# A decoder step: the first projection takes each chunk of tokens through all four channel panels, with both weight panels read side by side

## Chip, cores and metric

The kernel runs on one NeuronCore of a Trainium2 chip. The metric is the device time of one execution in microseconds; the median of the runs counts. The profile is of one further execution.

## The reference

One layer of a decoder for 1024 prompt tokens and 64 sample tokens (8 requests of 8 tokens), all in float32. The part that the change touches is the first 512 columns of the combined input projection, the pooling input `a`:

```python
def rms_norm(x, w):
    x32 = x.astype(F32)
    y = x32 * lax.rsqrt(jnp.mean(jnp.square(x32), axis=-1, keepdims=True) + EPS)
    return y.astype(x.dtype) * w

def project(x, ln1, w_in, q_norm, k_norm):
    p = jnp.einsum('btd,de->bte', rms_norm(x, ln1), w_in)
    a, q, k, v, g_a, g_b = jnp.split(p, IN_SPLITS, axis=-1)      # widths 512, 768, 768, 768, 1024, 1024
    ...
```

After it come the pooling of `a`, three groups of dilated attention, the gates, the output projection and an MLP of width 4096. They are the same before and after.

## The kernel before

**Layout.** Tokens lie along the free dimension (1088 columns), channels along the partitions, in eight k-tiles of 128 (`KD = 8`). The 1088 tokens are cut into three chunks of 384, 384 and 320 columns (`CHUNKS`). The 512 output channels of `a` are four panels of 128; two of them come from one weight panel `i["w_in"][0]` (called a0), two from `i["w_in"][1]` (a1). A weight panel is 128 x 2048 numbers: eight k-tiles of 256 output channels.

**Precision.** Every float32 operand is split into a high and a low part (type `F32R`), and a product is three passes (`PASSES`: high x high, high x low, low x high, weight part first). `split` makes the parts of a weight piece of 512 columns (two k-tiles): a copy on ScalarE (ACT, L116) for the high part, a subtraction on VectorE (DVE, L117) for the low one. `split_x` does the same with x, scaled by the norm's weight `ln1` (ACT L312, VectorE L313), into `act`.

**Buffers.** A weight piece lands in one of three `raw` buffers of 512 columns (`fetch`, L127), so the fourth piece cannot be asked for until the first has been split by both engines. The parts go into one of three `places`, each a whole panel. x lands in `xs`, twelve buffers for the three chunks of four pairs of k-tiles. All of these loads are issued by SyncE (SP) in one order. Accumulators are four PSUM banks.

**Order of the work.** TensorE's order is the program's. The other engines' instructions, SyncE's loads among them, are put in order by a planner that estimates when each can run; it may put a load that can go at once ahead of one that must wait for a buffer. `behind_pe` ties an instruction to the last matmul issued so far, so it can't run sooner.

**The stage.** Twelve small matmuls come first (`wu`). Then a0's four pieces are read (`panel` with `between=first`), after each the next pair of k-tiles of x for chunk 0. TensorE takes chunks 0, 1, 2 through a0 (`pool_input(0, ...)`: pairs of k-tiles, then passes, then the two output panels), and then chunks 0, 1, 2 through a1. After each chunk ACT copies the two accumulators into `ext` (`pool_evac`, L346 and L351). While TensorE works on a1, `x_sums(c)` multiplies the sums of squares of chunk c with a column of ones (L369), which gives the norm of each token; VectorE (L373, L375) and GpSimd (POOL, a power, L374) finish it. The squares are made by `square_x(c)` on ACT (L304), and POOL adds the four pairs of k-tiles with three adds for each chunk (L306). `sample_rows` copies the 64 sample columns with sixteen VectorE casts (L284). `wk` is a small transpose (L444). Right behind the stage stands the q projection of the sample tokens (`pq`, L632), which needs the casts, and the product `mt` (L405), which needs all norms. The next three weight panels (q, k, v) use the free place, then a0's, then a1's.

Of the kernel before, what the change touches and what calls it, by code (L numbers as in the profile page):

```python
# [7 lines left out]
F32 = mybir.dt.float32  # L8
F32R = mybir.dt.float32r
AF = mybir.ActivationFunctionType  # L10
ALU = mybir.AluOpType
# [4 lines left out]
P = 128  # L16
D = 1024
SEQ = 1024
NB, NT = 8, 8
TOK = SEQ + NB * NT  # L20
KD = D // P
CH = 384
# [5 lines left out]
HD = 64  # L28
# [9 lines left out]
def decoder_step(ctx, tc, i, o):  # L38
    nc = tc.nc
    v_, s_, g_, t_ = nc.vector, nc.scalar, nc.gpsimd, nc.tensor  # L40
    dma = nc.sync.dma_start
# [7 lines left out]
    def rr(p, shape, dt, name, tag, bufs):  # L49

        n = turn[p, tag] = turn.get((p, tag), -1) + 1
        return p.tile(shape, dt, name=name, tag=f"{tag}.{n % bufs}", bufs=1)
# [3 lines left out]
    cst = cp.tile([P, i["consts"].shape[1]], F32, name="cst")  # L56
# [8 lines left out]
    ident, m1, m3, halves, hmask, icnt, ms0, ms1, hsel, bsel = (take(n) for n in (128, 256, 128, 64, 1, 15, 136, 136, 4, 4))  # L65
    ln1, ln2, pscale, wqc = cols[:, 0:8], cols[:, 8:16], cols[:, 16:20], cols[:, 20:26]
# [24 lines left out]
    def part4(c):  # L91

        return slice(CHUNKS[c][0] // 4, (CHUNKS[c][0] + CHUNKS[c][1]) // 4)
# [12 lines left out]
    def from4(t, sub="p r l -> p l r"):  # L106
        return t.rearrange("p (r l) -> p r l", r=4).rearrange(sub)
# [7 lines left out]
    def split(dst_hi, dst_lo, src):  # L115
        ins = s_.activation(dst_hi, src, AF.Copy)  # L116
        v_.tensor_tensor(dst_lo, src, dst_hi.bitcast(F32), op=ALU.subtract)  # L117
        return ins

    def fetch(src, name, a, tied=False):  # L120
        raw = rr(wp, [P, 512], F32, name=f"raw_{name}_{a}", tag="raw", bufs=3)
        if callable(src):
            ins = dma(raw.rearrange("p (k n) -> p k n", k=4), src(a))
            if tied:
                behind_pe(ins)
        else:
            dma(raw, src[:, a:a + 512])  # L127
        return raw
# [35 lines left out]
    def panel(src, name, between=None, after=None):  # L164

        n = src.shape[1]
        wt = places[:, place[0] % 3]
        place[0] += 1
        for a in range(0, n, 512):
            raw = fetch(src, name, a)  # L170
            if between is not None:
                between(a // 512)
            ins = split(wt[:, 0, a:a + 512], wt[:, 1, a:a + 512], raw)
            if after is not None:
                behind_pe(ins, after[a // 512])
        throttle.append(ins)
        return wt

    def by_k(wt, kb=KD):
        return wt.rearrange("p s (k n) -> p s k n", k=kb)  # L180
# [69 lines left out]
    def acc_tile(name, tag="acc", bufs=4):  # L250
        return rr(acc_p, [P, 512], F32, name, tag, bufs)
# [17 lines left out]
    def win(name):  # L269
        return rr(xp, [P, LS], F32, name, "win", 2)  # L270
# [10 lines left out]
    def sample_rows():  # L281
        for s in range(2):
            for k in range(KD):
                behind_pe(v_.tensor_copy(smp_t[:, k, s * NS:(s + 1) * NS].rearrange("p (l r) -> p l r", r=4),  # L284
                                         act4[s][k][:, :, SEQ // 4:].bitcast(F32).rearrange("p r l -> p l r")))
    xs = {}

    def load_x(c, j):
        c0, n = CHUNKS[c]
        x = rr(xq, [P, 2, CH], F32, name=f"xs{c}_{j}", tag="xs", bufs=12)  # L290
        if c + j == 0:

            dma(x[:, 0, :n], i["xT"][:, 0, c0:c0 + n])
            dma(cols, i["cols"])
        else:
            dma(x[:, :, :n], i["xT"][:, 2 * j:2 * j + 2, c0:c0 + n])
        xs[c, "t", j] = x[:, :, :n]
        for k in range(2):
            xs[c, 2 * j + k] = x[:, k, :n]

    def square_x(c):
        t = [xs[c, "t", j] for j in range(4)]
        for j in (3, 0, 1, 2):
            behind_pe(s_.activation(t[j], t[j], AF.Square))  # L304
        for j in range(3):
            g_.tensor_tensor(t[3], t[3], t[j], op=ALU.add)  # L306

    def split_x(c, k):
        c0, n = CHUNKS[c]
        hi, lo = (act4[s][k][:, :, part4(c)] for s in range(2))  # L310
        x = xs[c, k].rearrange("p (l r) -> p r l", r=4)
        s_.activation(hi, x, AF.Copy, scale=ln1[:, k:k + 1])  # L312
        v_.scalar_tensor_tensor(lo, x, ln1[:, k:k + 1], hi.bitcast(F32), op0=ALU.mult, op1=ALU.subtract)  # L313

    def first(j):
        if j:
            load_x(0, j)
        else:
            dma(xs[0, 1], i["xT"][:, 1, :CH])
        split_x(0, 2 * j)  # L320
        split_x(0, 2 * j + 1)

    L = 15 + SEQ
    LS = L + NB * 23
    exts = {}

    def pool_input(ja, wt, c, middle=None):
        c0, n = CHUNKS[c]
        pts = [acc_tile(f"a{2 * ja + m}_{c}") for m in range(2)]
        for k in range(0, KD, 2):  # L330
            for p, (a, b) in enumerate(PASSES):
                for m in range(2):
                    for kk in (k, k + 1):
                        last_mm[0] = t_.matmul(  # L334
                            pts[m][:, :n], wt[:, a, kk, m * P:(m + 1) * P], act4[b][kk][:, :, part4(c)],
                            start=(p == 0 and kk == 0), stop=(p == 2 and kk == KD - 1))
            if middle and k == 4:
                middle()
        return pts

    def pool_evac(ja, c, pts):
        c0, n = CHUNKS[c]
        for m in range(2):
            ext = exts[2 * ja + m]
            npr = min(n, SEQ - c0)
            s_.copy(ext[:, 15 + c0:15 + c0 + npr].rearrange("p (l r) -> p l r", r=4),  # L346
                    from4(pts[m][:, :n])[:, :npr // 4])
            if npr < n:
                new = from4(pts[m][:, :n])[:, npr // 4:].rearrange("p (t q) r -> p q r t", q=2)
                for q in range(2):  # L350
                    s_.copy(ext[:, L:].rearrange("p (b t) -> p b t", b=NB)[:, 4 * q:4 * q + 4, 15:], new[:, q])  # L351

    def open_ext(g):
        exts[g] = rr(xp, [P, LS], F32, name=f"ext{g}", tag="ext", bufs=4)
        v_.memset(exts[g][:, :15], 0.0)
# [3 lines left out]
    for _ in range(12):  # L359
        t_.matmul(wu, ones, ones, start=True, stop=True)  # L360
    load_x(0, 0)
    wt = by_k(panel(i["w_in"][0], "a0", first))
    def x_sums(c):
        n = CHUNKS[c][1]
        rt = [rr(ps, [P, 1], F32, name=f"rt{c}_{b}", tag="rt", bufs=3) for b in range(3)]
        for b in range(3):
            w = min(P, n - b * P)
            for k in range(2):
                t_.matmul(rt[b][:w], xs[c, 6 + k][:, b * P:b * P + w], ones[:, :1], start=(k == 0), stop=(k == 1))  # L369
        for b in range(3):  # L370
            w = min(P, n - b * P)
            col = slice(3 * c + b, 3 * c + b + 1)
            v_.tensor_scalar(xms[:w, col], rt[b][:w], 1.0 / D, EPS, op0=ALU.mult, op1=ALU.add)  # L373
            g_.tensor_tensor(rtok[0][:w, col], xms[:w, col], mhalf[:w, :1], op=ALU.pow)  # L374
            v_.tensor_scalar(xeps[0][:w, col], xms[:w, col], EPS, None, op0=ALU.mult)  # L375
# [33 lines left out]
            v_.tensor_scalar(xeps[g][:, :8], xg, EPS, None, op0=ALU.mult)  # L409

    v_.memset(rtok[0], 0.0)
    for c in range(3):
        if c < 2:
            for j in range(4):
                load_x(c + 1, j)
        if c == 0:
            open_ext(0)
            open_ext(1)
        pool_evac(0, c, pool_input(0, wt, c))
        if c < 2:  # L420
            for k in range(KD):
                split_x(c + 1, k)
        if c:
            square_x(c - 1)
    square_x(2)
    w1 = by_k(panel(i["w_in"][1], "a1"))
    dma(cst, i["consts"])
    v_.tensor_scalar(wqs, wqc, HD ** -0.5, None, op0=ALU.mult)
    dma(states, i["stateT"].rearrange("g p b t -> p g (b t)"))
    kn = win("kn")[:, :P]  # L430
    for g in range(3):
        dma(kn[2 * g:2 * g + 2], i["qk_norm"][g, 1].rearrange("(j d) -> j d", j=2))
    open_ext(2)
    open_ext(3)
    for c in range(3):
        pool_evac(1, c, pool_input(1, w1, c, (lambda: x_sums(2)) if c == 2 else None))
        if c == 0:
            x_sums(0)
            sample_rows()
        if c == 1:  # L440
            x_sums(1)

            wk = rr(ps, [P, 512], F32, name="wk", tag="wu", bufs=1)[:, :6]
            t_.transpose(wk, kn[:6], ident[:6, :6])  # L444
            v_.tensor_tensor(wqk, wqs, wk, op=ALU.mult)
    moving = by_residue()
    next(moving)
    px.close()
# [722 lines left out]
    for g in (2, 1, 0):  # L1171
# [42 lines left out]
        for blks in ((8, 0), (1,), (2,), (3,), (4,), (5,)) + (((6, 7),) if g else ((6,), (7,))):  # L1214
# [12 lines left out]
            for js in (((0, 1), (2,)) if blks[0] in (1, 2, 3, 4, 5) else ((0,), (1,), (2,))):  # L1227
                for b in (blks[::-1] if g < 2 and js == (2,) and 8 in blks else blks):
# [4 lines left out]
                    def middle():  # L1233
                        step()
                        if own:
                            own_step(1)
# [1031 lines left out]
```

## Time and profile before

| | us |
|---|---|
| runs, median (lowest to highest of 3) | 1401.73 (1401.05 to 1402.97) |
| the profiled execution's own time | 1399.09 |
| its span, first to last instruction | 1397.3 |
| TensorE matmul busy | 1390.2 |
| VectorE, ACT, POOL busy | 954.0, 756.1, 258.3 |

The profile's page and its views give times in microseconds from the start of the span. PE is TensorE's matmuls, PEld its weight loads, DVE VectorE, ACT ScalarE, POOL GpSimd, SP SyncE (SPq: its queue, which issues loads). L334 is line 334 of the kernel. In a line of the order of time stand start, length, engine, line, operation, the names of what is written and read, the shape, the count, and in brackets the engine's idle time before it with what ended that. The chain that ended last goes back from the last instruction, at each step to what released it.

### The profile page before, as it was taken

Reading aid. Unit: us, or ns where it says so; the run is one execution under the profiler, and the core shown is the slowest. Engines: PE = TensorE matmul, PEld = TensorE weight load, DVE = VectorE, ACT = ScalarE, POOL = GpSimd, SP = SyncE. Lnnn points to the kernel's source line nnn. Section 1 sums busy time; section 2 is a strip of 40 time slices with the busy share of each in tenths; the row PEclk is TensorE's granted clock in tenths of the full one; section 3 lists DMA queues with packets and bytes.
Section 4 is the critical chain, followed back from the end, with each engine's and each line's share of the span. In section 5 each row is a group of like instructions: output and inputs, shape, how many; then the busy total and the mean of one; then the engine's idle time right before and its main releaser. Section 6 shows DMA issues by size and latency. Waiting matters only on the chain.

```text
span 1397.3 us, 29307 instructions
## 1 busy us (share of the span) xinstructions
PE 1390.2 (99%) x11101; PEld 1341.6 (96%) x11101; DVE 954.0 (68%) x1707; ACT 756.1 (54%) x1787; POOL 258.3 (18%) x362
## 2 busy tenths in 40 slices
PE   9999999999999999999999999999999999999998
PEld 8988987888999999999999999999999999999998
DVE  7788744776876776975559677765665686664565
ACT  8557875787764224554337454554554544444443
POOL 0854356676500000000010000000000000000100
PEclk9999999999999999999999999999999999999999
DMA  6456886755587777956369668765768987777674
GB/s 216 133 166 211 245 246 195 231 139 137 149 248 232 244 220 257 318 194 211 130 199 296 222 217 290 245 204 204 250 202 287 319 274 257 238 239 230 211 256 170
DMA packets 180445, 311.96 MB, mean 223 GB/s; under 512 B 26696, under 2 KB 82318, under 8 KB 178255
## 3 DMA queue, kind: packets, MB, share of 16 engines
q1 hardware_dynamic: 174670, 258.04, 57.8%
q0 software_dynamic: 5632, 52.04, 11.6%
q8 instruction: 87, 1.43, 0.4%
q14 instruction: 56, 0.45, 0.1%
HBM read 239.94 MB, written 122.12 MB: 259 GB/s over the span
## 4 chain that ended last, share of the span: by engine, by line
PE 98%; ACT 0%; DMA 0%; POOL 0%; SPq 0%; issue 0%; DVE 0%; DVEq 0%
PE pz L1330 24%; PE pd L2113 24%; PE pg L1330 12%; PE ph L205 7%; PE pqk L205 6%; PE pab L1330 5%; PE pv L205 5%; PE a L334 3%; PE pk L205 2%; PE pq L205 2%; PE sg0b L702 1%; PE pog0b L735 1%; PE pl L513 1%; PE tpg0b L721 1%; PE sg1b L702 0%; PE tpg1b L721 0%
## 5 line engine op out<-in xcount | busy, mean ns | idle before, releaser
L2113 PE MATMUL pd<-places 128*128 128x272 f32 x2688 | 331.7, 287 | 0.0
L2113 PEld LDWEIGHTS pd<-places 128*128 128x128 f32 x2688 | 331.6, 188 | 0.0
L116 ACT ACTIVATE places<-raw_d 128x544 fp32r<-128x544 f32 (+1 forms) x176 | 110.6, 646 | 159.1 <-DMA raw_d<-z_d 54.8
L2166 POOL DMA_DIRECT2D out_kv_sample_dram<-in_cache_kv_dram x96 | 46.9, 489 | 791.1 <-ACT places L116 582.2
L117 DVE TENSOR_TENSOR places<-raw_d,places 128x544 fp32r<-128x544 f32 (+1 forms) x176 | 122.4, 710 | 90.8 <-ACT places L116 89.0
L1330 PE MATMUL pz<-act,places 128*128 128x280 f32 (+1 forms) x1080 | 139.4, 287 | 0.0
L1330 PEld LDWEIGHTS pz<-act,places 128*128 128x128 f32 x1080 | 135.9, 188 | 0.0
L205 PE MATMUL ph<-act,places 128*128 128x280 f32 (+1 forms) x768 | 96.6, 287 | 0.0
L205 PEld LDWEIGHTS ph<-act,places 128*128 128x128 f32 x768 | 96.0, 188 | 0.1
L1330 PE MATMUL pg<-act,places 128*128 128x264 f32 (+1 forms) x576 | 75.6, 288 | 0.0
L1330 PEld LDWEIGHTS pg<-act,places 128*128 128x128 f32 x576 | 72.6, 188 | 0.6 <-issue 0.3
L1330 PE MATMUL pz<-places,apart 128*128 128x264 f32 (+1 forms) x528 | 67.9, 287 | 0.0
L1330 PEld LDWEIGHTS pz<-places,apart 128*128 128x128 f32 x528 | 66.6, 188 | 0.0
L205 PE MATMUL pqk<-places,act 128*128 128x512 f32 x240 | 60.6, 402 | 0.0
L1330 PE MATMUL pz<-act,apart 128*128 128x264 f32 (+1 forms) x456 | 59.1, 287 | 0.0
L1330 PEld LDWEIGHTS pz<-act,apart 128*128 128x128 f32 x456 | 57.5, 188 | 0.1
L661 POOL TENSOR_TENSOR mr<-ms,mhalf 128x4 f32<-128x4 f32 (+2 forms) x39 | 54.7, 1403 | 2.9 <-POOL ms L660 0.2
L205 PEld LDWEIGHTS pqk<-places,act 128*128 128x128 f32 x240 | 44.8, 192 | 9.6
L886 POOL TENSOR_TENSOR pck<-pck,qs 128x256 f32<-128x256 f32 x64 | 48.6, 791 | 21.1 <-DVE sta L711 12.4
L334 PE MATMUL a<-act,places 128*128 128x384 f32 (+1 forms) x288 | 50.5, 333 | 1.7 <-ACT act L312 1.1
L334 PEld LDWEIGHTS a<-act,places 128*128 128x128 f32 x288 | 47.6, 188 | 3.8 <-ACT act L312 1.9
L1330 PE MATMUL pab<-ab,places 128*128 128x264 f32 (+1 forms) x384 | 50.4, 286 | 0.0
(438 smaller groups left out, 2805.8 us busy)
## 6 DMA issues: line engine op xcount, KB each, us to landing
out_kv_sample_dram<-in_cache_kv_dram POOLq DMA_DIRECT2D x72, 480.0 KB, 5.0
raw_d<-z_d SPq DMA_DIRECT2D x112, 272.0 KB, 4.2
z_d<-t SPq DMA_DIRECT2D x80, 272.0 KB, 3.7
raw_d<-in_w_down_dram SPq DMA_DIRECT2D x80, 256.0 KB, 4.1
raw_u<-in_w_up_dram SPq DMA_DIRECT2D x64, 256.0 KB, 4.3
raw_qkv<-in_w_in_dram SPq DMA_DIRECT2D x36, 256.0 KB, 4.3
own_d<-in_cache_kv_dram POOLq DMA_DIRECT2D x32, 256.0 KB, 3.8
pck<-own_d SPq DMA_DIRECT2D x16, 512.0 KB, 4.8
```

The costliest lines, as they stand in the source:

```text
L116: ins = s_.activation(dst_hi, src, AF.Copy)
L117: v_.tensor_tensor(dst_lo, src, dst_hi.bitcast(F32), op=ALU.subtract)
L205: last_mm[0] = t_.matmul(out, lhs(a, k), rhs(b, k), start=(j == 0), stop=(j == len(terms) - 1))
L334: last_mm[0] = t_.matmul(pts[m][:, :n], wt[:, a, kk, m * P:(m + 1) * P], act4[b][kk][:, :, part4(c)], start=(p == 0 and kk == 0), stop=(p ...
L513: t_.matmul(pl[:, :npr], lin[:, g, :], dp_[:, c0:c0 + npr], start=True, stop=True)
L661: last_norm[0] = g_.tensor_tensor(r[:n, :H], ms[:n, :H], mhalf[:n, :H], op=ALU.pow)
L702: t_.matmul(sc[e][:, hp, j * P:(j + 1) * P], qT[rows, hp, :], kT[rows, 2 + hp, :], start=True, stop=True)
L721: t_.transpose(tp[:, hp * nk + j, :], sms[e][:, hp, j * P:(j + 1) * P], ident)
L886: ins = g_.tensor_tensor(out, *others, op=ALU.mult)
L1330: last_mm[0] = t_.matmul(out[c], lhs(*term), rhs(*term, c), start=(first and n == 0), stop=(n == len(terms) - 1), skip_group_check=not first)
L2113: last_mm[0] = t_.matmul(chain[t][c], A[:, a, t * P:(t + 1) * P], Z[:, b, c], start=(fresh and f == 0 and n == 0), stop=(f == NG - 1 and n ...
L2166: ins = g_.dma_start(d, a)
```

## The change

One loop over the three chunks takes the place of two. Both weight panels are read at the start, piece by piece in turn: a piece of a0, a piece of a1, and with them x of chunk 0 in eight loads of one k-tile each where before there were two single ones and three pairs. In chunk 0, TensorE takes k-tiles 0 to 3 in pairs through all four output panels, and then panel by panel the passes over k-tiles 4 to 7; in chunks 1 and 2 it goes panel by panel, each pass over all eight k-tiles. Each panel is copied out of PSUM when it is done (`pool_evac` takes one panel). The squares, the column sums, the sample casts and the small transpose are called from between the panels, by the table `THEN`: squares of chunk 0 after the second panel of chunk 1, those of chunk 1 after its fourth, those of chunk 2 and the casts after the first panel of chunk 2, the sums of chunks 0 and 1 after its second and third, and the sums of chunk 2 before the last pass of its fourth. The small loads (constants, state, key norms) come after chunk 0.

```diff
@@ -312,43 +312,71 @@
         s_.activation(hi, x, AF.Copy, scale=ln1[:, k:k + 1])
         v_.scalar_tensor_tensor(lo, x, ln1[:, k:k + 1], hi.bitcast(F32), op0=ALU.mult, op1=ALU.subtract)
 
-    def first(j):
-        if j:
-            load_x(0, j)
-        else:
-            dma(xs[0, 1], i["xT"][:, 1, :CH])
-        split_x(0, 2 * j)
-        split_x(0, 2 * j + 1)
+    def first_panels():
+        wts = []
+        for _ in range(2):
+            wts.append(places[:, place[0] % 3])
+            place[0] += 1
+        for j in range(4):
+            if j:
+                t = rr(xq, [P, 2, CH], F32, name=f"xs0_{j}", tag="xs", bufs=12)
+                xs[0, "t", j] = t
+                for k in range(2):
+                    xs[0, 2 * j + k] = t[:, k]
+                dma(t[:, 0], i["xT"][:, 2 * j, :CH])
+            raw = [fetch(i["w_in"][0], "a0", 512 * j)]
+            dma(xs[0, 2 * j + 1], i["xT"][:, 2 * j + 1, :CH])
+            raw.append(fetch(i["w_in"][1], "a1", 512 * j))
+            for ja in range(2):
+                split_x(0, 2 * j + ja)
+                ins = split(*(wts[ja][:, s, 512 * j:512 * j + 512] for s in range(2)), raw[ja])
+        throttle.append(ins)
+        return [by_k(w) for w in wts]
 
     L = 15 + SEQ
     LS = L + NB * 23
     exts = {}
 
-    def pool_input(ja, wt, c, middle=None):
+    BY_WEIGHT = ((0, 0), (1, 0), (0, 1))
+
+    def pool_input(c, then={}):
         c0, n = CHUNKS[c]
-        pts = [acc_tile(f"a{2 * ja + m}_{c}") for m in range(2)]
-        for k in range(0, KD, 2):
+        pts = {}
+
+        def mm(t, a, b, k, start, stop):
+            ja, m = divmod(t, 2)
+            if t not in pts:
+                pts[t] = acc_tile(f"a{t}_{c}")
+            last_mm[0] = t_.matmul(pts[t][:, :n], wt[ja][:, a, k, m * P:(m + 1) * P], act4[b][k][:, :, part4(c)],
+                                   start=start, stop=stop)
+
+        begun = 0 if c else 4
+        if c == 0:
+            for k in (0, 2):
+                for ja in range(2):
+                    for kk in (k, k + 1):
+                        for p, (a, b) in enumerate(PASSES if ja or kk == 0 else BY_WEIGHT):
+                            for m in range(2):
+                                mm(2 * ja + m, a, b, kk, kk == 0 and p == 0, False)
+        for t in range(4):
             for p, (a, b) in enumerate(PASSES):
-                for m in range(2):
-                    for kk in (k, k + 1):
-                        last_mm[0] = t_.matmul(
-                            pts[m][:, :n], wt[:, a, kk, m * P:(m + 1) * P], act4[b][kk][:, :, part4(c)],
-                            start=(p == 0 and kk == 0), stop=(p == 2 and kk == KD - 1))
-            if middle and k == 4:
-                middle()
-        return pts
-
-    def pool_evac(ja, c, pts):
+                for k in range(begun, KD):
+                    mm(t, a, b, k, c > 0 and p + k == 0, p == 2 and k == KD - 1)
+                if p == 1 and (t, 1) in then:
+                    then[t, 1]()
+            pool_evac(t, c, pts[t])
+            if t in then:
+                then[t]()
+
+    def pool_evac(t, c, pt):
         c0, n = CHUNKS[c]
-        for m in range(2):
-            ext = exts[2 * ja + m]
-            npr = min(n, SEQ - c0)
-            s_.copy(ext[:, 15 + c0:15 + c0 + npr].rearrange("p (l r) -> p l r", r=4),
-                    from4(pts[m][:, :n])[:, :npr // 4])
-            if npr < n:
-                new = from4(pts[m][:, :n])[:, npr // 4:].rearrange("p (t q) r -> p q r t", q=2)
-                for q in range(2):
-                    s_.copy(ext[:, L:].rearrange("p (b t) -> p b t", b=NB)[:, 4 * q:4 * q + 4, 15:], new[:, q])
+        ext = exts[t]
+        npr = min(n, SEQ - c0)
+        s_.copy(ext[:, 15 + c0:15 + c0 + npr].rearrange("p (l r) -> p l r", r=4), from4(pt[:, :n])[:, :npr // 4])
+        if npr < n:
+            new = from4(pt[:, :n])[:, npr // 4:].rearrange("p (t q) r -> p q r t", q=2)
+            for q in range(2):
+                s_.copy(ext[:, L:].rearrange("p (b t) -> p b t", b=NB)[:, 4 * q:4 * q + 4, 15:], new[:, q])
 
     def open_ext(g):
         exts[g] = rr(xp, [P, LS], F32, name=f"ext{g}", tag="ext", bufs=4)
@@ -359,7 +387,7 @@
     for _ in range(12):
         t_.matmul(wu, ones, ones, start=True, stop=True)
     load_x(0, 0)
-    wt = by_k(panel(i["w_in"][0], "a0", first))
+    wt = first_panels()
     def x_sums(c):
         n = CHUNKS[c][1]
         rt = [rr(ps, [P, 1], F32, name=f"rt{c}_{b}", tag="rt", bufs=3) for b in range(3)]
@@ -409,40 +437,31 @@
             v_.tensor_scalar(xeps[g][:, :8], xg, EPS, None, op0=ALU.mult)
 
     v_.memset(rtok[0], 0.0)
+    for g in range(4):
+        open_ext(g)
+
+    def key_norms():
+        wk = rr(ps, [P, 512], F32, name="wk", tag="wu", bufs=1)[:, :6]
+        t_.transpose(wk, kn[:6], ident[:6, :6])
+        v_.tensor_tensor(wqk, wqs, wk, op=ALU.mult)
+
+    THEN = ({}, {1: lambda: square_x(0), 3: lambda: square_x(1)},
+            {0: lambda: (square_x(2), sample_rows()), 1: lambda: x_sums(0), 2: lambda: (x_sums(1), key_norms()), (3, 1): lambda: x_sums(2)})
     for c in range(3):
         if c < 2:
             for j in range(4):
                 load_x(c + 1, j)
-        if c == 0:
-            open_ext(0)
-            open_ext(1)
-        pool_evac(0, c, pool_input(0, wt, c))
+        pool_input(c, THEN[c])
         if c < 2:
             for k in range(KD):
                 split_x(c + 1, k)
-        if c:
-            square_x(c - 1)
-    square_x(2)
-    w1 = by_k(panel(i["w_in"][1], "a1"))
-    dma(cst, i["consts"])
-    v_.tensor_scalar(wqs, wqc, HD ** -0.5, None, op0=ALU.mult)
-    dma(states, i["stateT"].rearrange("g p b t -> p g (b t)"))
-    kn = win("kn")[:, :P]
-    for g in range(3):
-        dma(kn[2 * g:2 * g + 2], i["qk_norm"][g, 1].rearrange("(j d) -> j d", j=2))
-    open_ext(2)
-    open_ext(3)
-    for c in range(3):
-        pool_evac(1, c, pool_input(1, w1, c, (lambda: x_sums(2)) if c == 2 else None))
         if c == 0:
-            x_sums(0)
-            sample_rows()
-        if c == 1:
-            x_sums(1)
-
-            wk = rr(ps, [P, 512], F32, name="wk", tag="wu", bufs=1)[:, :6]
-            t_.transpose(wk, kn[:6], ident[:6, :6])
-            v_.tensor_tensor(wqk, wqs, wk, op=ALU.mult)
+            dma(cst, i["consts"])
+            v_.tensor_scalar(wqs, wqc, HD ** -0.5, None, op0=ALU.mult)
+            dma(states, i["stateT"].rearrange("g p b t -> p g (b t)"))
+            kn = win("kn")[:, :P]
+            for g in range(3):
+                dma(kn[2 * g:2 * g + 2], i["qk_norm"][g, 1].rearrange("(j d) -> j d", j=2))
     moving = by_residue()
     next(moving)
     px.close()
```

## The prediction

> **What bounds the kernel now.** I read the page first, then the busy time by stage, then the chain that ended last, then each engine's order of time over the first 62 us.
>
> ```profile
> span 1397.3 us, 29307 instructions
> ...
> PE 1390.2 (99%) x11101; PEld 1341.6 (96%) x11101; DVE 954.0 (68%) x1707; ACT 756.1 (54%) x1787; POOL 258.3 (18%) x362
> ...
> L334 PE MATMUL a<-act,places 128*128 128x384 f32 (+1 forms) x288 | 50.5, 333 | 1.7 <-ACT act L312 1.1
> L334 PEld LDWEIGHTS a<-act,places 128*128 128x128 f32 x288 | 47.6, 188 | 3.8 <-ACT act L312 1.9
> ```
>
> TensorE is busy for all but 7.1 us. The changed projection is L334, 288 of 11101 matmuls, so the whole question is how its idle time moves. The stages show where TensorE idles (columns: stretch, its length, busy us and count by engine, granted clock, DMA share, GB/s):
>
> ```profile
> core 0: us, PE busy (x) PEld busy (x) DVE busy (x) ACT busy (x) POOL busy (x), PEclk, DMA share, GB/s
> 0.00:5.50 5.50, 4.44 (x24) 4.25 (x24) 1.42 (x9) 2.56 (x4) 0.20 (x4) 1.00 0.55 140
> 5.50:10.60 5.10, 3.39 (x14) 2.28 (x14) 3.24 (x5) 4.01 (x6) 0.00 (x0) 1.00 0.99 352
> 10.60:61.10 50.50, 50.50 (x313) 49.73 (x314) 42.55 (x79) 38.42 (x63) 23.83 (x16) 1.00 0.48 157
> 61.10:400.00 338.90, 338.77 (x2749) 292.91 (x2747) 232.47 (x609) 239.20 (x942) 183.75 (x243) 1.00 0.64 191
> 400.00:1397.30 997.30, 993.12 (x8008) 992.41 (x8004) 674.35 (x1008) 471.93 (x775) 50.48 (x100) 1.00 0.73 237
> ```
>
> From 10.6 to 61.1 us the stage has no idle at all, and the rest of the program does not touch the change. What can be won lies before 10.6 us. Start us, length, and what, from the chain, give the pace:
>
> ```profile
> 10.55 30.90 PE a L334 x179
> 41.45 1.23 PE rt L369 x12
> 42.68 8.59 PE a L334 x48
> ...
> 52.50 0.15 PE wk L444
> 52.65 5.48 PE a L334 x36
> 58.13 1.11 PE rt L369 x12
> ...
> 61.19 0.12 PE pq L632
> ```
>
> A 384-column matmul takes 8.59/48 = 0.179 us, a 320-column one 5.48/36 = 0.152. The stage's work is 192 x 0.179 + 96 x 0.152 = 34.4 + 14.6 = 49.0 us, and the three column sums and the transpose (1.23 twice, 1.11, 0.15) are 3.7: together 52.7.
>
> ```profile
> 6.09 0.44 PE L334 MATMUL a<-act,places 128*128 128x384 f32 x1 [0.59 <-ACT places L116]
> 6.98 2.46 PE L334 MATMUL a<-act,places 128*128 128x384 f32 x11 [0.45 <-ACT act L312]
> 9.68 0.44 PE L334 MATMUL a<-act,places 128*128 128x384 f32 x1 [0.24 <-ACT act L312]
> 10.55 30.90 PE L334 MATMUL a<-act,places 128*128 128x384 f32 x179 [0.42 <-ACT act L312]
> ```
>
> From the first matmul at 6.09 to the next projection at 61.19 are 55.1 us, so 2.4 are lost; 13 matmuls stand in the 4.46 us before 10.55, which is 2.1 of it. **The most that a perfect start could bring is 2.4 us, 0.17% of the time.** About 0.2% (2.8 us) is what a measurement of this kernel can tell from no change.
>
> **The change part by part.** It keeps all 288 matmuls, 24 splits of x, 8 splits of weight pieces, 12 squares, 9 POOL adds, 36 sums. It changes their order and the loads.
>
> *First matmul.* It needs x 0, the scale columns and the first weight piece, the first three loads before and after:
>
> ```profile
> 1.66 0.43 SPq L127 DMA_DIRECT2D raw_a<-in_w_in_dram  x1
> 2.60 0.43 SPq L127 DMA_DIRECT2D raw_a<-in_w_in_dram  x1
> ...
> 4.08 0.95 SPq L296 DMA_DIRECT2D xs<-in_xT_dram  x2
> 6.79 0.34 SPq L127 DMA_DIRECT2D raw_a<-in_w_in_dram  x1
> ```
>
> ```profile
> 5.41 0.63 ACT L116 ACTIVATE places<-raw_a 128x512 fp32r<-128x512 f32 x1 [1.02 <-DMA raw_a<-in_w_in_dram]
> ...
> 7.24 0.63 ACT L116 ACTIVATE places<-raw_a 128x512 fp32r<-128x512 f32 x1 [0.31 <-DMA raw_a<-in_w_in_dram]
> 8.65 1.85 ACT L312 ACTIVATE act<-xs,cols 128x384 fp32r<-128x384 f32 x2 [0.77 <-DMA xs<-in_xT_dram]
> ```
>
> ```profile
> 6.07 0.69 DVE L117 TENSOR_TENSOR places<-raw_a,places 128x512 fp32r<-128x512 f32 x1 [0.74 <-ACT places L116]
> ```
>
> So it stays at 6.09. Zero.
>
> *k-tiles 0 to 3, all four panels.* Each pair of k-tiles now feeds 24 matmuls (4.3 us) instead of 12 (2.1), against ACT's two x splits (1.85) and two weight splits (1.26): 3.1. TensorE becomes the slower side. The third weight piece lands at 7.24 whatever panel it belongs to; it is wanted 12 matmuls in, at 8.2. x 2 lands no later than the pair did (8.65), wanted at 10.4. The fourth piece has three raw buffers ahead of it: the first comes free when VectorE ends its split, 6.07 + 0.69 = 6.76, and SyncE issues at 6.79 (the row). At the first piece's issue to landing (1.66 to 5.41, 3.75 us) it is there at 10.5, split by 12, wanted at 12.5. I charge 0.1 us; 48 matmuls end at 14.8.
>
> *k-tiles 4 to 7.* Here is the new wait. Eight pieces go through three buffers, and a round trip is 6.76 - 1.66 = 5.1 us. The seventh piece (panel 0, k-tiles 6 and 7) waits for the fourth's split, about 12.1, lands 3.2 to 3.75 later, at 15.3 to 15.9, and is split by 16.5 at the latest; x 7 stands right behind it on SyncE and its split follows, 16.6 to 17.4. The first run of the new order asks for k-tile 6 at 15.2 and 7 at 15.3, so TensorE waits 1.3 to 2.1 us; its low part costs another 0.2. Which end is told by the rate of the loads:
>
> ```profile
> 4.00:6.00 2.00, 1.50 (x12) 1.31 (x11) 0.91 (x1) 0.98 (x3) 0.00 (x0) 1.00 0.91 251
> ...
> 8.00:10.00 2.00, 1.76 (x8) 1.31 (x8) 0.94 (x2) 1.35 (x2) 0.00 (x0) 1.00 1.06 397
> ```
>
> The 3.75 was measured at 251 GB/s; by then they run at 397, so I take 1.3. With 0.1 and 0.2 the start loses **1.6 us instead of 2.4: a gain of 0.8.** Ends: 0 (gain 2.4) and 3.7 (loss 1.3, the x loads ahead of the pieces, below).
>
> *Chunk 1.* Its first eight matmuls want all eight k-tiles within 1.4 us of 24.9, the eighth at 26.1. ACT, free of weights at about 17.5, needs 8 x 0.9 for the splits (1.85 for two) plus three evacuations of about 0.4: done at 25.9. Covered by 0.2 us; without that cover up to 0.8. I take 0.
>
> *Squares and sums.* They move back: gates at the second and fourth panel of chunk 1 and the first of chunk 2, where they were at panel-0 ends near 26 and 33.
>
> ```profile
> 30.63 3.05 ACT L304 ACTIVATE xs<-xs 128x768 f32<-128x768 f32 x4
> ```
>
> ```profile
> 32.30 16.72 POOL L306 TENSOR_TENSOR xs<-xs,xs 128x768 f32<-128x768 f32 x8 [31.85 <-ACT xs L304]
> 49.73 2.55 POOL L374 TENSOR_TENSOR stats<-stats,mhalf 128x1 f32<-128x1 f32 x3 [0.71 <-DVE stats L373]
> 52.25 2.32 POOL L306 TENSOR_TENSOR xs<-xs,xs 128x640 f32<-128x640 f32 x1
> ```
>
> Before, the last add ended at 54.6 and the last sums ran at 58.1: 3.5 us spare. After: chunk 0 ends at 6.09 + 17.2 + 1.6 = 24.9, chunk 1 at 42.1, the panels of chunk 2 (3.65 each) with two sums bring the last sums to 58.1 again. POOL starts chunk 1's adds 1.67 us after their gate, at 43.7; six adds of 2.09 end at 56.3, 1.8 us ahead. If the three powers of the first sums (2.55) get ahead of the last add, as in the rows, it is 58.8: 0.7 lost, 1.4 with the 0.71 that POOL waits for VectorE. With the second sums' powers ahead too, another 2.55 and 0.71: 4.7. One trip in front is the nearest row, but a POOL that stands in adds without a break has less reason for it than the one that ran out of them at 49.0; I take 0 and keep 4.7 for the range.
>
> *VectorE.* It shares something with POOL:
>
> ```profile
> 34.24 4.64 DVE L117 TENSOR_TENSOR places<-raw_a,places 128x512 fp32r<-128x512 f32 x2 [2.55 <-ACT places L116]
> 47.52 2.07 DVE L284 CAST smp_t<-act 128x64 fp32r<-128x64 f32 x5
> ```
>
> While POOL adds, a 0.69 us split takes 2.3, and the first cast waits out an add. The 16 sample casts now start at 45.7, amid adds: one to each add leaves ten after 56.3, under 2 us, and the first sample matmul comes at about 60.4, so zero. The key panel's place comes free only at 49.4 (was 33), wanted near 66; the value panel's at 58 to 60, wanted near 72: eight splits, even at 2.3 us, are in time.
>
> [...]
>
> **Sum:** 2.4 - 1.6 = 0.8 us off the profiled execution: span 1396.5, its own time 1399.09 to 1398.3. The median of the runs stands 2.6 above that execution: 1401.73 - 0.8 = **1400.9**.
>
> **The rivals.**
> *Fully covered start.* The late piece comes in time and nothing is lost after 6.09: 1401.7 - 2.4 = 1399.3. For it: all DMA at 397 GB/s would bring chunk 0's 3.7 MB by about 14. Against: the buffer round trip.
> *Weights behind x.* SyncE's rows show both pair loads at 4.08 issued ahead of the piece that waited till 6.79. If four single x loads (0.2 MB each, 0.5 us at 397 GB/s) get ahead of the pieces, the seventh comes 2 us later: 1402.9.
> *The sums come late* (slower). Place: the last sums on TensorE at 58.1, behind POOL's ninth add. It costs from the moment that this add ends after 58.1, and is a measurable loss once it ends after 61.7. One trip of powers ahead: 1401.6 to 1402.3; two: 1405.6.
> *Single loads move slower.* If chunk 0's eight x loads (1.57 MB) ran at the 251 GB/s of the time when singles were in flight, not 397, they would take 6.3 us, not 4.0: 2.3 later, 1403.2. Against: loads overlap, 352 GB/s from 5.5 on already. [...]
>
> **How the numbers follow.** Forecast (within 0.6 of 1400.9) 0.42, covered start 0.12, one trip 0.18, two trips 0.10, weights behind x 0.11, slow singles 0.07. The range 1399.0 to 1403.6 leaves out the two trips and some of the covered start and slow singles. Faster by over 0.2% (under 1398.9) needs the covered start and something more from the rest of the program, whose 4.3 idle us after 61.1 may shift: 0.08. Slower: 0.12. Within: 0.80.
>
> **What would show it.** First L334 matmul still at 6.1; no gap over 0.3 us until about 14.8; then gaps before k-tiles 6 and 7 that sum to 1.3 to 1.6, ended by ACT's splits or their loads; chunk 1 without a gap; POOL's ninth add ended by 58; first pq at about 60.4 instead of 61.2. The prediction is wrong if the last sums wait for POOL, if the gap at k-tiles 6 and 7 is over 3 us, or if the rest of the program moves by itself.

## The result, and the profile after

| | before | after |
|---|---|---|
| runs, median (lowest to highest) | 1400.17 us (1398.92 to 1402.97, 6 runs) | 1411.51 us (1410.42 to 1415.63, 6 runs) |
| ratio after/before, 95% interval | | 1.0084 [1.0067, 1.0102] |
| the profiled execution's own time | 1399.09 us | 1415.63 us |
| first q projection (`pq`) on TensorE | 61.03 us | 71.67 us |

The change makes the kernel 0.84% slower; 1400.9 and at most 1403.6 were forecast. The profiled execution of after is the slowest of the six, so its part behind the stage (5.9 us more lost) is not typical; the medians differ by 11.34 us. The 10.64 us at the stage's end are the loss to explain.

The page of after: TensorE's work is the same 11101 matmuls, but the projection (now L350) has 8.6 us of idle time ahead of it where it had 1.7, and its matmuls got longer (345 ns for 333). The clock row begins with an 8: in the first of its 40 slices TensorE was granted 0.8 to 0.9 of its clock.

```profile
span 1413.9 us, 29314 instructions
...
PE 1396.4 (99%) x11101; PEld 1346.2 (95%) x11101; DVE 952.5 (67%) x1707; ACT 756.3 (53%) x1787; POOL 257.6 (18%) x362
...
PEclk8999999999999999999999999999999999999999
...
L350 PE MATMUL a<-act,places 128*128 128x384 f32 (+1 forms) x288 | 52.6, 345 | 8.6 <-ACT places L116 8.6
```

TensorE's order of time in after (start, length, what, count, idle before it and its releaser):

```profile
6.36 9.26 PE L350 MATMUL a<-act,places 128*128 128x384 f32 x50 [0.72 <-ACT places L116]
23.46 34.48 PE L350 MATMUL a<-act,places 128*128 128x384 f32 x190 [7.83 <-ACT places L116]
57.78 1.39 PE L397 MATMUL rt<-ones,xs 128*128 128x1 f32 x12
...
68.09 1.35 PE L397 MATMUL rt<-ones,xs 128*128 128x1 f32 x12 [1.38 <-DVE stats L401]
69.37 2.50 PE L350 MATMUL a<-act,places 128*128 128x320 f32 x8
71.67 0.42 PE L651 MATMUL pq<-places,smp_t 128*128 128x256 f32 x1
```

Three things are seen. The first 50 matmuls run without a wait, as wanted; by 15.62 TensorE has done as many as took till 17.85 before. Then it stands for 7.83 us at k-tile 6, for a weight piece's split on ACT. And the last column sums wait for VectorE, after which eight matmuls take 2.50 us, as long as sixteen should.

What holds the piece is on SyncE and on ACT (after; L296 loads a pair of chunk 1, L127 a weight piece, L312 splits x, L116 splits a piece):

```profile
9.74 0.43 SPq L296 DMA_DIRECT2D xs<-in_xT_dram  x1
10.33 0.35 SPq L127 DMA_DIRECT2D raw_a<-in_w_in_dram  x1
10.73 1.91 SPq L296 DMA_DIRECT2D xs<-in_xT_dram  x3
12.74 0.84 SPq L127 DMA_DIRECT2D raw_a<-in_w_in_dram  x1
15.34 0.33 SPq L127 DMA_DIRECT2D raw_a<-in_w_in_dram  x1
```

```profile
17.05 0.62 ACT L116 ACTIVATE places<-raw_a 128x512 fp32r<-128x512 f32 x1
17.57 5.32 ACT L312 ACTIVATE act<-xs,cols 128x384 fp32r<-128x384 f32 x6
22.79 1.13 ACT L116 ACTIVATE places<-raw_a 128x512 fp32r<-128x512 f32 x2
```

The seventh and eighth piece must wait for one of three raw buffers. Chunk 1's loads and splits need no such buffer, so the planner put all four pair loads ahead of the seventh piece's load (12.74) on SyncE, and chunk 1's eight splits ahead of the last two pieces' splits on ACT. ACT takes its list in that order: x of chunk 1, which TensorE wants from about 25 us, is split first, and the pieces that TensorE stands for come at 22.79.

The clock falls too (stretches of after; the number right behind POOL's busy time is the granted clock):

```profile
15.65:18.10 2.45, 0.00 (x0) 0.00 (x0) 2.24 (x4) 2.45 (x4) 0.00 (x0) 1.00 1.06 385
18.20:28.30 10.10, 4.84 (x15) 4.85 (x16) 7.51 (x12) 6.96 (x11) 0.00 (x0) 0.50 0.93 312
...
69.40:72.70 3.30, 3.30 (x14) 3.30 (x14) 2.46 (x8) 1.01 (x4) 2.66 (x4) 0.50 0.77 207
```

From 18.2 to 28.3 TensorE is granted half its clock: the 15 matmuls of that stretch take 4.84 us, 0.32 each, for 0.18. It happens again from 69.4 to 72.7. In the kernel before the clock is 1.00 from before the first of these matmuls to the end of the work.

### The profile page after: what moved, and what is told of

It is laid out like the page before. It is cut to its first block, busy times and chain, and to the rows that moved or that the text cites. A ratio compares the mean times of both kernels' runs of the same rounds, so it can differ in the third digit from the quotient of the medians.

```text
span 1413.9 us, 29314 instructions
## 1 busy us (share of the span) xinstructions
PE 1396.4 (99%) x11101; PEld 1346.2 (95%) x11101; DVE 952.5 (67%) x1707; ACT 756.3 (53%) x1787; POOL 257.6 (18%) x362
## 4 chain that ended last, share of the span: by engine, by line
PE 70%; DMA 1%; DVE 1%; SPq 1%; ACT 0%; issue 0%; DVEq 0%; ACTq 0%
PE pd L2132 23%; PE pz L1349 23%; PE pg L1349 11%; PE ph L205 7%; PE pab L1349 4%; DMA raw_ab<-in_w_ab_dram 1%; DMA u<-u_d 0%; PE pog0b L754 0%; PE sg0b L721 0%; DMA gg<-g_d 0%; PE tpg0b L740 0%; SPq L1646 0%; PE pk L205 0%; PE pv L205 0%; DVE places L117 0%
## 5 line engine op out<-in xcount | busy, mean ns | idle before, releaser
L116 ACT ACTIVATE places<-raw_d 128x544 fp32r<-128x544 f32 (+1 forms) x176 | 110.6, 646 | 161.8 <-DMA raw_d<-z_d 67.4
L350 PE MATMUL a<-act,places 128*128 128x384 f32 (+1 forms) x288 | 52.6, 345 | 8.6 <-ACT places L116 8.6
L350 PEld LDWEIGHTS a<-act,places 128*128 128x128 f32 x288 | 50.8, 200 | 9.4 <-ACT places L116 9.1
```

What stands on the lines that cost most here:

```text
L350: last_mm[0] = t_.matmul(pts[t][:, :n], wt[ja][:, a, k, m * P:(m + 1) * P], act4[b][k][:, :, part4(c)], start=start, stop=stop)
```

## The experiments

Changes are to the kernel after, unless said otherwise. The time of before stands beside each group, from the same chip.

**First group** (before: 1399.67 us).

*ACT's order.* Chunk 1's and 2's splits of x are tied on ACT behind the last weight split.

```diff
-        s_.activation(hi, x, AF.Copy, scale=ln1[:, k:k + 1])
+        made = s_.activation(hi, x, AF.Copy, scale=ln1[:, k:k + 1])
+        if c:
+            in_front(made, throttle[0])
```

> The changed kernel, with the splits of x of chunks 1 and 2 tied on ACT behind the last weight split; SyncE's order of loads stays. Theory (order): TensorE's gap of 7.8 us at k-tile 6 comes from eight chunk 1 splits ahead of the last two weight splits on ACT; but SyncE also asks for 1.6 MB of chunk 1 x ahead of the seventh piece, so that piece lands near 20 and the gap shrinks only to about 5 us, the clock still drops, and chunk 1's later splits cost up to 2: 1409 to 1411. Rival (buffers): the seventh piece itself is not there before 22.8, ACT's order only follows it: gap still 7.8, 1411.5 or more. Were ACT's order the whole cause: gap under 2, about 1403.

1411.7 us, 1.0080 [1.0065, 1.0095]: as slow as after. TensorE's order:

```profile
20.66 15.20 PE L352 MATMUL a<-act,places 128*128 128x384 f32 x70 [5.18 <-ACT places L116]
37.49 20.26 PE L352 MATMUL a<-act,places 128*128 128x384 f32 x120 [1.64 <-ACT ext L377]
```

ACT's split of the seventh piece:

```profile
19.97 0.63 ACT L116 ACTIVATE places<-raw_a 128x512 fp32r<-128x512 f32 x1 [2.98 <-DMA raw_a<-in_w_in_dram]
```

The gap falls from 7.83 to 5.18, as expected, so ACT's order is a part only: ACT now idles 2.98 us for the seventh piece, which SyncE issued at 12.66 behind the pair loads of chunk 1. Much of what is won comes back: the splits of chunk 1 now end so late that TensorE waits at 37.49 for a copy of an accumulator queued behind splits, and `pq` comes at 70.59, only 1.08 us earlier than in after.

*ACT's and SyncE's order.* Besides, the loads of chunks 1 and 2 wait for VectorE's split of the fifth piece.

```diff
-        v_.tensor_tensor(dst_lo, src, dst_hi.bitcast(F32), op=ALU.subtract)
+        lows.append(v_.tensor_tensor(dst_lo, src, dst_hi.bitcast(F32), op=ALU.subtract))
...
+            if c:
+                in_front(ins, lows[4])
```

> As the run before, and the loads of x of chunks 1 and 2 also wait for VectorE's split of the fifth weight piece, so that SyncE asks for pieces seven and eight first; still three raw buffers. Theory (order): the seventh piece, asked for near 12.5, lands near 16, gap at most 1.5 us, no drop of the clock, first pq 8 to 9 us earlier than the 71.7 of the changed kernel: about 1403. Rival (buffers): three buffers alone hold the seventh piece back, gap 4 us or more with a drop of the clock: about 1408.

1407.79 us, 1.0051 [1.0036, 1.0066]. TensorE's order:

```profile
17.34 9.43 PE L355 MATMUL a<-act,places 128*128 128x384 f32 x52 [2.21 <-ACT places L117]
...
62.84 1.46 PE L402 MATMUL rt<-ones,xs 128*128 128x1 f32 x12 [1.76 <-DVE stats L406]
```

The gap is 2.21 us and the clock stays whole through it (the 52 matmuls behind it take 9.43 us, 0.18 each); `pq` starts at 66.53 instead of 71.67. SyncE issues the seventh piece at 12.63, no sooner than in the run before (12.66), but its split starts at 16.66 instead of 19.97: the pair loads cost by being in flight ahead of the piece, not by holding up its issue. The 2.21 is what the round trip of three buffers costs with chunk 1 out of the way (the constants and the state are still issued ahead of the piece, from 9.26 on), where 1.3 to 2.1 was forecast. The time is the one named for the rival, 1408, though not by its mechanism: chunk 1's x now comes late (waits of 0.56 and 0.42 at 27.32 and 28.19), the sums wait 0.42 and 1.76, and the clock halves from 63.9 to 67.3 (`pq`'s first matmuls take 0.41 us, those from 67.37 on 0.28).

*Buffers of their own.* The fourth to seventh piece get buffers of their own; nothing is tied.

```diff
+    def own_raw(src, name, j, n):
+        if n < 3 or n == 7:
+            return fetch(src, name, 512 * j)
+        if n < 5:
+            raw = xq.tile([P, 512], F32, name=f"rawx_{n}", tag=f"rawx.{n}", bufs=1)
...
+        dma(raw, src[:, 512 * j:512 * j + 512])
+        return raw
...
-            raw = [fetch(i["w_in"][0], "a0", 512 * j)]
+            raw = [own_raw(i["w_in"][0], "a0", j, 2 * j)]
```

> The changed kernel with pieces four to seven in buffers of their own, so that no weight piece waits for a buffer; no tie. Both theories: the planner has no reason to put chunk 1 ahead, no gap at k-tile 6, no drop of the clock there: first pq near 61 to 62, about 1401 to 1403. If buffers were the cause it is better than the run before by over 2.5 us, if the order was, within 1.5 of it. The late wait of the last sums stays in either.

1403.98 us, 1.0027 [1.0017, 1.0038]. TensorE's order:

```profile
16.40 32.50 PE L364 MATMUL a<-act,places 128*128 128x384 f32 x189 [0.43 <-ACT act L312]
...
59.53 1.35 PE L411 MATMUL rt<-ones,xs 128*128 128x1 f32 x12 [1.75 <-DVE stats L415]
```

With no piece waiting for a buffer, the planner puts the pieces ahead of chunk 1 by itself, on both queues, and the gap is gone. So the buffer wait is the cause of the order, and with it of the gap. The run is 3.8 us faster than the one before, more than the 2.5 that was to point to the buffers. Against before, the median falls from 11.3 us over to 4.3. The late wait stays, and with it a halved clock (0.50) from 61.9 to 65.3.

*Clock kept up.* The kernel after with 36 idle products of `ones` in front of k-tile 4, which fill the gap.

```diff
+        for _ in range(36 if c == 0 else 0):
+            t_.matmul(wu, ones, ones, start=True, stop=True)
```

> The changed kernel with 36 extra small matmuls on TensorE behind k-tile 3, which nobody waits for and which fill most of the 7.8 us gap. Theory (clock): the gap's end stays near 23.5 (set by the weight split), but the clock stays at 1.0 and the 15 matmuls behind it take 0.174 and not 0.320 us: 2.2 us less, about 1409.3. Rival: the halved clock hides behind other waits, no change: 1411.5.

1409.91 us, 1.0065 [1.0050, 1.0080]. The same stretch as above, and TensorE's order:

```profile
18.20:28.30 10.10, 9.42 (x70) 9.09 (x70) 9.87 (x16) 10.09 (x13) 0.00 (x0) 1.00 0.91 311
```

```profile
24.25 32.35 PE L350 MATMUL a<-act,places 128*128 128x384 f32 x190 [0.68 <-ACT places L116]
...
69.30 0.28 PE L653 MATMUL pq<-places,smp_t 128*128 128x256 f32 x1
```

The clock is whole (1.00). From the gap's end to the first sums the same 190 matmuls take 32.18 us (24.25 to 56.43) for 34.32 in after: the halved clock cost 2.1 us there. The distance to before is 1.1 us less than after's by the medians, and the two intervals overlap, so the 2.1 rests on the one profile.

**Second group** (before: 1400.08 us): what makes the last sums late, on top of the version with buffers of its own. Two things are varied: the powers of the norms on POOL are tied behind its ninth add, and the sixteen sample casts on VectorE come right behind chunk 2's splits, untied.

```diff
-            g_.tensor_tensor(rtok[0][:w, col], xms[:w, col], mhalf[:w, :1], op=ALU.pow)
+            in_front(g_.tensor_tensor(rtok[0][:w, col], xms[:w, col], mhalf[:w, :1], op=ALU.pow), last_add[2])
```

```diff
-    {0: lambda: (square_x(2), sample_rows()), ...
+    {0: lambda: square_x(2), ...
...
+            if c == 1:
+                sample_rows()
```

*Powers late.*

> The run with own buffers, with all powers of the sums tied on POOL behind the ninth add. In the run with own buffers the last sums started at 59.5 where TensorE was ready at 57.6, and the clock halved from 61.9 to 65.3. Theory (POOL order): the first sums' powers, which stand ahead of the last two adds, cause it; with them behind, the adds end near 55.5, no wait at the last sums, no halved clock, first pq at 58.5 to 59: 3 us less, about 1401. Rival (VectorE): the wait is for the buffers of the second sums, which VectorE reads late because POOL's adds and the casts hold it: it waits as long or longer, 1404.

1406.39 us, 1.0044 [1.0032, 1.0056]: 6.3 us over before, where buffers alone left 4.3. POOL, VectorE and TensorE:

```profile
39.17 15.89 POOL L308 TENSOR_TENSOR xs<-xs,xs 128x768 f32<-128x768 f32 x9 [38.72 <-ACT xs L306]
```

```profile
46.17 9.93 DVE L284 CAST smp_t<-act 128x64 fp32r<-128x64 f32 x16 [8.21 <-PE a L366]
56.02 0.15 DVE L417 TENSOR_SCALAR stats<-rt 128x1 f32<-128x1 f32 x1
```

```profile
56.31 2.50 PE L413 MATMUL rt<-ones,xs 128*128 128x1 f32 x12 [1.80 <-DVE stats L417]
```

POOL's adds now run without a break, and VectorE's casts between them take 9.93 us for 16; the first sums, made at 49.5, are read at 56.02. The sums have three PSUM buffers (`rt`), one for each block of 128 tokens, so the second sums cannot begin until the first are read: the wait has moved one chunk forward, as the rival said, and the clock halves (0.50) from 56.9 to 63.7.

*Casts early.*

> The run with own buffers, with the 16 sample casts called behind chunk 2's splits, untied, so that VectorE does them before POOL's adds begin; POOL's order as the planner makes it (powers ahead of the last two adds). Theory (POOL order): the powers start as soon as the first sums are there, the last add still comes behind three of them, last sums wait about 1 us instead of 1.9: about 1403. Rival (VectorE): with the casts gone VectorE reads the sums at once, no wait, no halved clock: about 1401.

1402.55 us, 1.0016 [1.0007, 1.0024]. TensorE's order:

```profile
59.03 1.38 PE L411 MATMUL rt<-ones,xs 128*128 128x1 f32 x12 [0.84 <-POOL xs L306]
```

VectorE's part of the wait is gone, and what remains is POOL's: 0.84 us for the ninth add, behind the first powers. The clock still halves, from 61.3 to 64.7 (`pq`'s first matmuls take 0.41 us, those from 64.79 on 0.28).

*Both.*

> Both of the two before. All theories: no wait at the last sums, no halved clock in the stage, first pq at 58.5 to 59.0 where the kernel before has 61.0. If the stage is all that counts, 2.0 to 2.5 us under the kernel before: about 1397.5. If the rest of the program loses 2 to 4 us by itself whenever the order of the other engines is planned anew, as in the four runs so far: 1399.5 to 1401.

1400.38 us, 1.0010 [0.9998, 1.0022]. TensorE's order, and the group of casts (ns each: least, median, most):

```profile
15.90 32.81 PE L366 MATMUL a<-act,places 128*128 128x384 f32 x189 [0.43 <-ACT act L314]
48.56 1.39 PE L413 MATMUL rt<-ones,xs 128*128 128x1 f32 x12
...
57.33 1.27 PE L413 MATMUL rt<-ones,xs 128*128 128x1 f32 x12
...
59.81 0.28 PE L669 MATMUL pq<-places,smp_t 128*128 128x256 f32 x1
```

```profile
L284 DVE CAST smp_t<-act x16: 199/206/211, 26.1 to 34.2; 128x64 fp32r<-128x64 f32 x16
```

No wait is left at the sums, the clock is 1.00 through the stage, and `pq` starts at 59.81: 1.22 us before the kernel before, and 0.8 later than the upper end expected. Neither edit alone does this; both together bring the median from 4.3 us over before (buffers alone) to 0.3 (one of its eleven executions took 1409.03). The time lies where it was put for the case that the rest of the program loses what the stage wins.

*Pairs.* The last version, with chunk 0 loaded as before: two single loads and three pairs.

> The run before with x of chunk 0 loaded as in the kernel before (two single k-tiles, then three pairs) and everything else kept. If the single k-tiles are what makes the start dense, x 2 and 3 land up to 1 us later and the start loses 0.5 to 1 us more than with singles. If the start is dense because each k-tile feeds four panels, no difference: first pq within 0.3 us of the run before.

1400.51 us, 1.0001 [0.9993, 1.0010]. TensorE's order:

```profile
16.80 32.24 PE L367 MATMUL a<-act,places 128*128 128x384 f32 x190 [0.93 <-ACT places L116]
...
60.46 0.28 PE L670 MATMUL pq<-places,smp_t 128*128 128x256 f32 x1
```

`pq` 0.65 us later, inside what was named for single loads making the start dense: single loads are no slower here, in this one profile a little better. The first matmul alone starts 0.16 later, and the medians can't tell.

**Third group** (before: 1400.22 us): why a stage that is 1.2 us shorter doesn't show in the time. Followed matmul by matmul, the version with both edits stays 1.25 us ahead of before till 274 us, is 0.8 ahead at 347, and 0.65 behind at 374. VectorE there, in before and in that version, and then TensorE in the same two:

```profile
349.39 0.18 DVE L1105 TENSOR_REDUCE sfm<-osm 128x4 f32<-128x12 f32 x1 [1.95 <-DMA osm<-so_d]
349.49 1.55 DVE L611 CAST natt<-act 128x256 fp32r<-128x256 f32 x4
```

```profile
349.80 0.17 DVE L1142 TENSOR_REDUCE sfm<-osm 128x4 f32<-128x12 f32 x1 [3.16 <-DMA osm<-so_d]
349.89 2.55 DVE L648 CAST natt<-act 128x256 fp32r<-128x256 f32 x4
```

```profile
363.85 3.06 PE L205 MATMUL pq<-places,natt 128*128 128x256 f32 x24
```

```profile
363.09 1.65 PE L205 MATMUL pq<-places,natt 128*128 128x256 f32 x12
365.37 2.18 PE L205 MATMUL pq<-places,natt 128*128 128x256 f32 x12 [0.63 <-DVE natt L648]
```

VectorE stands at the reduction `sfm` for a load that lands no sooner (349.80 for 349.39) though TensorE is 0.8 us ahead, with the casts of the next rows (`natt`) behind it. The two runs move this one reduction behind those casts, in that version and in the kernel before.

```diff
-        v_.tensor_reduce(mm, nm.rearrange("p g h -> p h g"), axis=AX.X, op=ALU.min)
+        behind_pe(v_.tensor_reduce(mm, nm.rearrange("p g h -> p h g"), axis=AX.X, op=ALU.min))
```

> The version with own buffers, early casts and late powers, and one VectorE instruction moved: the first reduction of the sample outputs (`sfm`), which waited 3.16 us for a load there (till 349.80) with the casts of q's next rows (`natt`) queued behind it, is tied to the matmul that stands ahead of its use. Theory (the 1.2 us that this version gains by 61 us are eaten because VectorE, standing behind a load that doesn't come sooner, gives TensorE its rows 0.6 + 0.8 us late at 365): VectorE has no wait for `osm` near 350, the casts start near 348.5, TensorE has no wait for `natt` at 365, it stays 0.8 us ahead of the kernel before at 375 where it was 0.65 behind, and the median falls by 1.4, to about 1399.0, ratio 0.9990 to 0.9997. Rival (VectorE and POOL are simply full between 350 and 367, 13.45 of 15 us, so another wait of the same size comes in the place): still 0.5 to 0.7 us behind at 375 and 1400.4.

> The kernel before with the same single instruction moved, nothing else. There VectorE waited 1.95 us for the load (till 349.39), but TensorE had no wait for `natt` at 365. Theory: no change, 1400.1, ratio 0.9995 to 1.0005, the pace of TensorE is the same within 0.1 us to the end. Rival (the instruction's place is worth something by itself): 1399.4 or less.

With both edits: 1400.21 us, 1.0002 [0.9993, 1.0011]. In the kernel before: 1400.38 us, 1.0002 [0.9993, 1.0011]. VectorE, then TensorE, in the first:

```profile
348.44 0.40 DVE L648 CAST natt<-act 128x256 fp32r<-128x256 f32 x1 [1.10 <-PE pv L205]
```

```profile
363.73 3.06 PE L205 MATMUL pq<-places,natt 128*128 128x256 f32 x24
```

In this execution the step goes as the theory said: the casts start at 348.44, TensorE has no wait at 365 and keeps its place between 347 and 374, 0.1 us ahead of before at both. The median did not follow (1399.0 was expected, and 1400.4 by the rival). This execution had lost 0.95 us already near 100 us, where TensorE waited 0.7 for VectorE (`pl`), though up to there the program is that of the version with both edits, which had no such wait. In the kernel before, the moved reduction had nothing to win, and its one profile drifts by 1.5 us too. Executions differ by about 1 us in such places; a gain of that size is below what these runs resolve, so that this wait is what eats the gain is not shown by the time. No version here beats the kernel before.

## Why the prediction was wrong

**Where the 10.64 us are.** Against the version that has none of the waits, row by row: the first matmul starts 0.32 later (6.36 for 6.04); the gap is 7.40 longer (7.83 for 0.43); from there to the first sums 1.49 (34.32 us for 190 matmuls, 32.66 for 189 and 0.17 for one more), the halved clock (2.14 against the run with the gap filled); from the first sums to `pq` 2.64 (13.89 for 11.25), the late sums and the clock behind them. Together 11.85, and the two `pq` differ by 11.86. That version is 1.22 ahead of before, which leaves 10.64.

**k-tiles 0 to 3: right.** Zero for the first matmul (6.36 in after, 6.04 to 6.49 in the experiments), 48 matmuls without a wait, and 2.2 us won by 15.6. One reading was off without harm: the row at 7.24 is the second piece's split, not the third's, and it is the second that is wanted 12 matmuls in.

**k-tiles 4 to 7: the step that failed.** "x 7 stands right behind it on SyncE and its split follows": it was taken that the seventh piece, once its buffer came free, had only its round trip ahead of it. In the trace it had four pair loads of chunk 1 ahead on SyncE and chunk 1's eight splits on ACT. With both ties the wait is 2.21, just above the upper end given for this step; so the round trip was sized about right and the queues were missed. By the two runs with ties, the 7.83 are 2.65 for ACT's order (7.83 to 5.18), 2.97 for chunk 1's loads in flight ahead of the piece (5.18 to 2.21), and 2.21 for the three buffers, of which the run with buffers of their own leaves 0.43. The rival "weights behind x" named this mechanism, but only on SyncE, with chunk 0's single loads, and at 2 us: ACT's queue, where the splits of a later chunk stood ahead (5.32 us in one row), was not counted. The profile of before had the hint that the prediction itself used, loads at 4.08 issued ahead of a piece that waited till 6.79.

**The clock: not in the sum.** It is 1.00 in every quoted stretch of before, and no term asked what a gap of some us does to it. It cost 2.1 us behind the long gap. In the trace of after it went from 1.00 to 0.50 at 18.15, 2.5 us after the end of the last matmul (15.62), and back to 1.00 at 28.39, 4.9 us after the restart at 23.46 (more in the last section).

**The sums: the rival came, mostly by another engine.** "I take 0 and keep 4.7 for the range" for POOL; "so zero" for VectorE's casts. The place (the last sums) and the size of one trip (0.7 to 1.4) are near what came, 1.38 in after and 1.75 with buffers of its own, but that is luck: what ended the wait in both was VectorE. POOL's own part was 0.84 once VectorE's was taken away (casts early). In after:

```profile
52.98 7.10 POOL L306 TENSOR_TENSOR xs<-xs,xs 128x768 f32<-128x768 f32 x4 [2.81 <-ACT xs L304]
```

```profile
54.46 7.07 DVE L284 CAST smp_t<-act 128x64 fp32r<-128x64 f32 x16 [14.55 <-PE a L350]
...
65.94 1.94 DVE L117 TENSOR_TENSOR places<-raw_qkv,places 128x512 fp32r<-128x512 f32 x1 [1.01 <-ACT places L116]
67.80 0.14 DVE L401 TENSOR_SCALAR stats<-rt 128x1 f32<-128x1 f32 x1
```

The casts were costed by their own consumer (`pq`), which they did not delay. Behind them in VectorE's queue stand splits of the next panel and the reading of the sums, and behind that, by the three `rt` buffers, TensorE's next sums. Sixteen casts of 206 ns (3.3 us) took 7.07 us beside four adds, and a split of 0.69 took 1.94. Behind the late sums the clock was halved once more, which cost about 1 us by `pq` (13.89 us from the first sums for 12.87 in the run with the gap filled, where the same wait left the clock whole) and more behind it. With the casts moved early VectorE's part of the wait vanishes, and with the powers late as well POOL's, and the halved clock with them.

**Slow single loads, chunk 1.** Neither cost anything that shows: pairs were not faster, and with the pieces in time chunk 1 runs without a gap.

**The rest of the program.** It was left out of the sum, with the warning that the forecast fails if it moves by itself. It does: in one execution each, after and the versions of the first two groups lose 0.8 to 2 us between 347 and 375, all but the one with the filled gap. VectorE's wait at the `sfm` load goes with it: 1.95 us in before and 1.91 with the gap filled, 2.95 to 3.67 in the eight that lose. That it is the cause was tested in one version, and there the time did not show it. After's other losses, near 110, 320, 580 and 750 us in its slowest execution, were not tested and stay open.

## What to carry to other kernels

When a loop order makes more loads wait for the same few buffers, ask what the scheduler will put in their place on every queue that the late piece must pass: not the wait for the buffer, but work that needs no buffer, hoisted ahead of it on SyncE and on ACT, was the cost here (7.8 us for 2.2). Cost a moved batch on an engine by what is queued behind it, not only by its own consumer, and add the price of a halved clock to each gap on TensorE, in after 2.1 us behind a gap of 7.8 and about 1 us behind one of 1.4. A gain of 1 us early in a long kernel reaches the end only if no later wait is set by something that does not come sooner.

## What was not expected of the hardware

TensorE's clock was halved (18.15 us in after) 2.5 us after the end of its last matmul (15.62) and stayed so 4.9 us into full work again (23.46 to 28.39). It was halved as well, for 3.4 us (69.35 to 72.76), after a stretch that was never idle longer than 1.4 us. With the same late wait (1.38 us) in the run with filled gap it was not halved.

The 7 us that end 1.25 us after the last sums' start, and the stretch behind them, in after:

```profile
62.34:69.34 7.00, 5.62 (x45) 5.34 (x43) 5.88 (x17) 2.23 (x6) 6.30 (x7) 1.00 0.46 123
69.40:72.70 3.30, 3.30 (x14) 3.30 (x14) 2.46 (x8) 1.01 (x4) 2.66 (x4) 0.50 0.77 207
```

The same in the run with the gap filled:

```profile
61.00:68.00 7.00, 5.62 (x45) 5.34 (x43) 6.00 (x17) 2.23 (x6) 6.31 (x7) 1.00 0.46 124
68.00:72.00 4.00, 4.00 (x34) 3.98 (x34) 3.33 (x12) 1.07 (x4) 4.00 (x6) 1.00 0.77 237
```

TensorE is busy for the same 5.62 us with the same 45 matmuls in both; behind them the clock is 0.50 in the one and 1.00 in the other. The same wait of 1.38 us cost a halved clock in the one execution and none in the other, so its length does not tell the two apart. What tells them apart was not shown: no run varied it by itself.
